# Differential attention on one core: keys and queries transposed in full precision and split afterwards, scores from three products over 64 rows, and a new order of the unit

## The chip, the cores and the metric

The kernel runs on 1 core of one Trainium2 chip. The metric is the device time of one execution in microseconds (us). The engines are named as in the profile: PE (TensorE, with PEld for its weight loads), DVE (VectorE), ACT (ScalarE), POOL (GpSimd) and SP, which only issues transfers here. Each engine works through its own instructions in the order in which the program has them; semaphores tie the engines together.

## What is computed

Two layers of a transformer with 1024 latent tokens and 256 context tokens of width 1024. In each layer one input projection feeds a Fourier mixer, a pooling mixer and differential attention; an output projection and a gated residual follow. The change lies in the attention, of which the reference says:

```python
def diff_attend(q, k, v, lam):
    s = jnp.einsum('bhmqd,bhmkd->bhmqk', q, k).astype(jnp.float32) * (QK_DIM ** -0.5)
    p = jax.nn.softmax(s, axis=-1)
    p = p[:, :, 0] - lam * p[:, :, 1]
    return jnp.einsum('bhqk,bhkd->bhqd', p.astype(v.dtype), v)
```

There are 4 heads; each has two maps (m = 0, 1) with queries and keys of 64 values, and values of 128. Before this, q and k are normalized (RMS over 64) and rotated. All inputs are float32.

## The kernel before

float32 data goes through TensorE in a reduced one-pass form (F32R). Where precision matters, a number is kept as hi + lo, two F32R parts, and a product is made of several matmuls that add up in PSUM: hi with hi, hi with lo, lo with hi.

**Stages of a layer**: projections for the gates and the mixers (whose work is not touched here), then the token-wise projections `proj_tok` in chunks of 256 columns: K0, K1, Q0, Q1, V0, V1. Each chunk works through pairs of token tiles (5 pairs for K and V); a pair takes 48 matmuls of 256 columns into one PSUM tile and then calls `post`, which issues the work on the result. Then attention runs in units.

**Keys**: `qk_post` normalizes and rotates a pair; one pair later `qk_late` scales it and writes, per head and map, `[hi | lo]` side by side into `ks` (128 tokens x 128). During the V chunks `k_trans` turns `ks` into `kT[2h+m]`, hi in rows 0 to 63 and lo in rows 64 to 127: 24 groups of up to four F32R transposes per layer, up to five groups behind each V pair (`v_chunk`). **Queries** go to DRAM (`qd`) and come back by query tile (`q_load`). For each unit `q_split` builds `[hi | lo | hi]` with three DVE instructions (L878 to L880) and `q_trans` makes four F32R transposes and one ACT copy (L892, L899).

**A unit** is one head of one tile of 128 queries against 1280 keys: 8 tiles x 4 heads, 32 units per layer. The first layer has two more, in which a context tile's four heads go together over 256 keys. `units` lists them, and `step(i)` issues for unit i (`cur`) its scores, row minima (the scores are negated) and exponentials, and for the units before it what comes later: `combine` (i-1) joins the two maps' exponentials, `p_trans` transposes the result in groups of 4, 4 and 2 tiles and `pv` multiplies by the values (i-2), `sub_norm` and `z_out` normalize and gate (i-2, i-3). When a query tile's four heads are done, `z_trans` and `z_low` transpose and split the gated result, and `out_proj` multiplies it by the output weights in pieces (`PIECES`, `ENDS`: first column, width, and how many steps after the last head).

`score(u, m)` makes one map: two products over all 128 rows, f = 0 and 1, in chunks of 512, 512 and 256 columns, 6 matmuls, so 12 in a unit. In `step` the two maps stand apart: scores of map 0 and its minimum first; transposes for the next unit, scores of map 1 and its minimum behind them.

**What sets the order**: the schedule is manual, each engine's queue is the order in which the code calls it. Two pools bind the engines: PSUM tiles `S` for scores (2 buffers, 3 banks each) and `x` for everything else (8 buffers up to the first V chunk, 2 from then on). A tile can be written again when its last reader is done.

## Time and profile before

| | us |
|---|---|
| median of 3 runs | 1451.82 (1447.77 to 1453.87) |
| profiled execution | 1448.99 |
| its span, first to last instruction | 1447.0 |
| first layer, minimum of unit 2 to minimum of unit 33 | 256.5 |
| second layer, minimum of unit 2 to minimum of unit 31 | 220.3 |
| PE busy in the span | 1381.8 (95%) |
| DVE busy in the span | 979.2 (68%) |

The profiled execution lies 2.8 us under the median of the runs. A matmul's end is modelled and includes the time to its result, so the pace of matmuls is read from start to start, not from their durations. "x6" in a row of the timeline means that six instructions in a row are merged; "[0.58 <-ACT t L938]" means that the engine sat idle for 0.58 us before, until that instruction released it.

### The profile page before, as it was taken

Reading aid. Unit: us, or ns where it says so; the run is one execution under the profiler, and the core shown is the slowest. Engines: PE = TensorE matmul, PEld = TensorE weight load, DVE = VectorE, ACT = ScalarE, POOL = GpSimd, SP = SyncE. Lnnn points to the kernel's source line nnn. Section 1 sums busy time; section 2 is a strip of 40 time slices with the busy share of each in tenths; the row PEclk is TensorE's granted clock in tenths of the full one; section 3 lists DMA queues with packets and bytes.
Section 4 is the critical chain, followed back from the end, with each engine's and each line's share of the span. In section 5 each row is a group of like instructions: output and inputs, shape, how many; then the busy total and the mean of one; then the engine's idle time right before and its main releaser. Section 6 shows DMA issues by size and latency. Waiting matters only on the chain.

```text
span 1447.0 us, 24063 instructions
## 1 busy us (share of the span) xinstructions
PE 1381.8 (95%) x9364; PEld 1240.6 (86%) x9364; DVE 979.2 (68%) x1553; ACT 567.6 (39%) x1230; POOL 775.9 (54%) x827
## 2 busy tenths in 40 slices
PE   7899999899999998999999899999999999999998
PEld 1688899779999987888888778988999998888887
DVE  2853366886895178798898654573464319989896
ACT  2632212101232265666665433121131227656663
POOL 2543222456785057667677842226887107766664
PEclk9899999999999999999999999999999999999999
DMA  9220242575123032112113321526412202111110
GB/s 354 101 90 32 85 149 91 187 266 166 60 88 117 1 103 81 66 45 74 45 45 112 104 66 38 205 80 213 148 44 85 78 22 67 45 45 45 59 59 30
DMA packets 65153, 137.07 MB, mean 95 GB/s; under 512 B 7312, under 2 KB 19728, under 8 KB 65040
## 3 DMA queue, kind: packets, MB, share of 16 engines
q1 hardware_dynamic: 49712, 108.82, 22.5%
q10 hardware_dynamic: 15328, 26.72, 5.3%
q8 instruction: 74, 1.21, 0.3%
q14 instruction: 39, 0.32, 0.1%
HBM read 105.63 MB, written 29.88 MB: 94 GB/s over the span
## 4 chain that ended last, share of the span: by engine, by line
PE 46%; DVE 21%; POOL 7%; issue 3%; ACT 2%; DMA 2%; ACTq 0%; POOLq 0%; SPq 0%; DVEq 0%
PE x L360 16%; DVE sm L923 6%; PE S L913 6%; PE x L1056 6%; PE x L993 5%; PE x L340 5%; PE x L753 3%; DVE e L1020 3%; PE x L977 2%; DVE t L952 1%; DVE t L980 1%; POOL e L759 1%; POOL sm L803 1%; DVE t L210 1%; PE x L892 1%
## 5 line engine op out<-in xcount | busy, mean ns | idle before, releaser
L360 PE MATMUL x<-wh,t 128*128 128x256 f32 x2432 | 445.9, 285 | 0.1
L360 PEld LDWEIGHTS x<-wh,t 128*128 128x128 f32 x2432 | 381.7, 192 | 1.8 <-issue 1.0
L360 PE MATMUL x<-wl,t 128*128 128x256 f32 x1216 | 344.7, 283 | 0.0
L923 DVE TENSOR_REDUCE sm<-S 128x1 f32<-128x1280 f32 (+1 forms) x132 | 194.8, 1476 | 72.2 <-PE S L913 72.0
L360 PEld LDWEIGHTS x<-wl,t 128*128 128x128 f32 x1216 | 233.7, 192 | 1.3 <-issue 1.2
L913 PE MATMUL S<-t,e 128*128 128x512 f32 (+1 forms) x768 | 180.9, 371 | 2.8 <-ACT e L899 1.4
L340 PE MATMUL x<-t,wh 128*128 128x512 f32 (+1 forms) x640 | 173.3, 381 | 8.8 <-DVE t L289 4.3
L938 ACT ACTIVATE t<-S,sm 128x1280 f32<-128x1280 f32 (+1 forms) x140 | 171.7, 1230 | 1.2 <-DVE sm L923 1.2
L993 PE MATMUL x<-t,t 128*128 128x128 f32 x1312 | 157.5, 275 | 3.3 <-DVE t L980 2.7
L993 PEld LDWEIGHTS x<-t,t 128*128 128x128 f32 x1312 | 153.7, 192 | 6.4 <-DVE t L980 2.9
L913 PEld LDWEIGHTS S<-t,e 128*128 128x128 f32 x768 | 126.3, 190 | 20.6 <-ACT t L938 2.0
L340 PEld LDWEIGHTS x<-t,wh 128*128 128x128 f32 x640 | 114.1, 192 | 31.6 <-POOL t L289 5.4
L318 POOL TENSOR_TENSOR wl<-st,wh 128x1024 fp32r<-128x1024 f32 x36 | 93.1, 2587 | 84.3 <-ACT wh L317 83.6
L961 POOL TENSOR_TENSOR t<-t,t 128x768 f32<-128x768 f32 (+1 forms) x64 | 116.2, 1816 | 5.3
L317 ACT ACTIVATE wh<-st 128x1024 fp32r<-128x1024 f32 x64 | 64.8, 1059 | 138.4 <-DMA xpart<-e 45.8
L977 PE MATMUL x<-ident,t 128*128 128x128 f32 x636 | 101.2, 274 | 5.7 <-DVE e L1059 4.1
L953 POOL TENSOR_SCALAR t<-t,sm 128x768 f32<-128x768 f32 x62 | 83.4, 1344 | 42.8 <-DVE sm L949 26.6
L753 PE MATMUL x<-wh,t 128*128 128x512 f32 x288 | 93.6, 404 | 8.5 <-DVE t L528 4.7
L1056 PE MATMUL x<-wh,e 128*128 128x512 f32 (+1 forms) x312 | 98.9, 384 | 2.6 <-ACT e L899 1.0
L340 PE MATMUL x<-t,wl 128*128 128x512 f32 (+1 forms) x320 | 100.2, 374 | 0.0
L210 DVE SCALAR_TENSOR_TENSOR t<-t,sc,t 128x512 f32<-128x512 f32 x98 | 90.8, 968 | 1.5 <-DMA t<-in_wmB_dram 1.1
L977 PEld LDWEIGHTS x<-ident,t 128*128 128x128 f32 x636 | 75.1, 141 | 15.9 <-DVE e L1059 4.5
(224 smaller groups left out, 2318.0 us busy)
## 6 DMA issues: line engine op xcount, KB each, us to landing
st<-in_w_in_dram SPq DMA_DIRECT2D x48, 512.0 KB, 4.0
t<-in_wmB_dram ACTq DMA_DIRECT2D x24, 512.0 KB, 5.4
xpart<-e ACTq DMA_DIRECT2D x36, 256.0 KB, 3.8
t<-xpart SPq DMA_DIRECT2D x18, 512.0 KB, 3.9
t<-in_wmS_dram SPq DMA_DIRECT2D x16, 512.0 KB, 8.5
st<-in_w_out_dram SPq DMA_DIRECT2D x16, 512.0 KB, 5.1
t<-in_x_dram SPq DMA_DIRECT2D x10, 512.0 KB, 10.3
e<-in_x_dram SPq DMA_DIRECT2D x20, 256.0 KB, 4.5
```

Source lines behind the costliest of these rows:

```text
L210: dve.scalar_tensor_tensor(a, w, sk, a, MULT, ADD)
L318: lo_eng[hf].tensor_tensor(lo[:, sl, :], st, hi[:, sl, :].bitcast(F32), SUB)
L340: pe.matmul(p[:, :m], lhsT=W[wi][:, k, ct * 128:ct * 128 + 128], rhs=H[k][hi][:, c0:c0 + m], start=(n == 0), stop=(n == 3 * KT - 1))
L360: pe.matmul(bank[:, i * 256:i * 256 + 256], lhsT=H[k][hi][:, j * 128:j * 128 + 128], rhs=W[wi][:, k, :], start=(n == 0), stop=(n == 3 * KT ...
L753: pe.matmul(ps, lhsT=zr[k][zi][:, j * 128:j * 128 + 128], rhs=W[wi][:, k, :], start=(n == 0), stop=(n == 11))
L913: pe.matmul(S[:, i * nk + c:i * nk + c + n], lhsT=s["qT"][i][:, m * 2 + f, :], rhs=kT[2 * h + m][:, k0 + c:k0 + c + n], start=(f == 0), st ...
L923: dve.tensor_reduce(nb, S[:, :nh * nk].rearrange("p (h k) -> p h k", h=nh), AX.X, ALU.min)
L938: act.activation(p[:, sl], S[:, sl], AF.Exp, bias=nb[:, i:i + 1], scale=-1.0, accum_out=ls[:, i:i + 1])
L961: pool.tensor_tensor(p[0][:, cut:end], p[0][:, cut:end], p[1][:, cut:end], ADD)
L977: pe.transpose(ps[:, i * 128:i * 128 + 128], s["p"][0][:, (t0 + i) * 128:(t0 + i + 1) * 128], ident)
L993: pe.matmul(o[:, i * 128:i * 128 + 128], lhsT=s["PT"][:, i * nkt + t, :], rhs=vv[h][:, kt0 + t, :], start=(t == 0), stop=(t == nkt - 1))
L1056: pe.matmul(ps[:, :m], lhsT=zz[:, k, :], rhs=Wa[hf][wi][:, k, w0:w0 + m], start=(n == 0), stop=(n == 11))
```

## The change

1. `qk_late` no longer splits the keys; it puts the scaled pair into a list. A new `k_trans`, called at the start of the next `qk_post`, makes four float32 transposes of it (both maps of a head lie in one 128x128 block), then ACT writes the hi part and DVE the lo part straight into `KH[h]` and `KL[h]`: rows 0 to 63 are map 0, rows 64 to 127 map 1. The transposes in the V chunks, `ks`, `identR`, `q_split` and the `qs` tiles are gone.
2. `q_trans` is called once per query tile, not per unit: four float32 transposes, one ACT copy (hi), one DVE subtraction (lo).
3. `score` makes both maps together: three products (hi hi, hi lo, lo hi) over 64 rows each, the two maps in turn, 18 matmuls in a unit instead of 12. The built program gives the matmuls of map 0 the rows 0 to 63 of the array and those of map 1 the rows 64 to 127.
4. `step` has another order, `out_proj` four pieces of 256 columns, one in each of the steps 2 to 5 after a tile's last head, and `z_trans` and `z_low` move to the end of a step. The gates (`g_load`) are loaded four steps later. `e2` has 10 buffers instead of 9.

```diff
-    e2p = tc.alloc_tile_pool(name="e2", bufs=9)
+    e2p = tc.alloc_tile_pool(name="e2", bufs=10)
...
+        def k_trans():
+            if later:
+                p, c, t1 = later.pop(0)
+                ps = PX()
+                for hh in range(2):
+                    for i in range(2):
+                        o = (2 * hh + i) * 128
+                        pe.transpose(ps[:, o:o + 128], t1[:, i, 2 * hh:2 * hh + 2, :].rearrange("p m e -> p (m e)"), ident)
+                for hh in range(2):
+                    hi, lo = [K[2 * c + hh][:, 256 * p:256 * p + 256] for K in (KH, KL)]
+                    b = ps[:, 256 * hh:256 * hh + 256]
+                    act.activation(hi, b, AF.Copy)
+                    dve.tensor_tensor(lo, b, hi.bitcast(F32), SUB)
...
-                for m in range(4):
-                    kd = ks[4 * c + m][:, 2 * p:2 * p + 2, :]
-                    act.activation(kd[:, :, 0:64], t1[:, :, m, :], AF.Copy)
-                    (dve if m % 2 else pool).tensor_tensor(kd[:, :, 64:128], t1[:, :, m, :], kd[:, :, 0:64].bitcast(F32), SUB)
+                else:
+                    later.append((p, c, t1))
...
+        def q_trans(j):
+
+            ps = PX()
+            for h in range(NH):
+                pe.transpose(ps[:, h * 128:h * 128 + 128], st[j]["q"][:, h * 128:h * 128 + 128], ident)
+            hi, lo = parts(j)
+            act.activation(hi.rearrange("p a b -> p (a b)"), ps, AF.Copy)
+            dve.tensor_tensor(lo.rearrange("p a b -> p (a b)"), ps, hi.rearrange("p a b -> p (a b)").bitcast(F32), SUB)
+            st[j]["Q"] = hi, lo
...
+                for n, (q, k) in enumerate(((0, KH), (0, KL), (1, KH))):
                     for c in range(0, nk, 512):
...
+                        w = min(512, nk - c)
+                        for m in range(2):
+                            r = slice(64 * m, 64 * m + 64)
+                            pe.matmul(S[m][:, i * nk + c:i * nk + c + w], lhsT=Q[q][r, h, :],
+                                      rhs=k[h][r, k0 + c:k0 + c + w], start=(n == 0), stop=(n == 2))
...
-        PIECES = [(0, 512, 2), (512, 512, 3)]
-        ENDS = {} if full else {6: [(0, 256, 3), (256, 256, 5), (512, 256, 5), (768, 256, 6)],
-                                7: [(0, 512, 2), (512, 256, 3), (768, 256, 3)]}
+        PIECES = [(c, 256, 2 + c // 256) for c in range(0, D, 256)]
+        LAST = {7: [(0, 512, 2), (512, 512, 3)]} if full else {7: [(0, 512, 2), (512, 256, 3), (768, 256, 3)]}
+        ENDS = () if full else (6, 7)
...
-                for _ in range(5):
-                    if k_groups:
-                        k_trans(*k_groups.pop(0))
```

The new body of `step`, in its three parts (what is left out in the third are the output pieces that are due):

```python
            if old:
                p_trans(old, 0)
                p_trans(old, 4)
            if prev and i > 1:
                combine(prev)
            if cur:
                score(cur)
            if old:
                p_trans(old, 8)
            if cur:
                row_max(cur, 0)
                row_max(cur, 1)
            if done:
                z_out(done)
            yield
            ...
            if cur:
                expo(cur, 0)
            if old:
                pv(old)
            if cur:
                expo(cur, 1)
            if old:
                sub_norm(old)
            yield
            ...
            if 1 in fin:
                z_trans(fin[1])
                z_low(fin[1])
            if i + 1 < N and units[i + 1][1] in (0, -1):
                q_trans(units[i + 1][0])
```

PE in the second layer, before, at the end of one step and the start of the next, in a step without an output piece (L977 transposes for PV, L913 scores, L892 query transposes, L993 PV, `x` and `S` the PSUM tiles):

```order
L977 MATMUL x_14108<-ident,t_2409_13936 128x128 x2
L993 MATMUL x_14120<-t_1893_11492,t_2441_14060 128x128 x10
L977 MATMUL x_14136<-ident,t_2434_14037 128x128 x4
L913 MATMUL S_14142<-t_1925_11808,e_2447_14087 128x512 x2
L913 MATMUL S_14142<-t_1925_11808,e_2447_14087 128x256
L913 MATMUL S_14142<-t_1925_11808,e_2447_14087 128x512 x2
L913 MATMUL S_14142<-t_1925_11808,e_2447_14087 128x256
L977 MATMUL x_14149<-ident,t_2434_14037 128x128 x4
L1026 MATMUL x_14155<-ident,e_2236_13264 128x128 x4
L892 MATMUL x_14171<-identR,qs_14113 128x128 x4
```

PE in the second layer, after, at the end of a step with `z_trans` (L1007) and the start of the next (L1036 the output piece, L958 transposes for PV, L894 scores):

```order
L1036 MATMUL x_14470<-wh_12536,e_2329_14103 128x256
L1036 MATMUL x_14470<-wl_12537,e_2329_14103 128x256
L1036 MATMUL x_14470<-wh_12536,e_2330_14104 128x256
L1007 MATMUL x_14487<-ident,e_2297_13963 128x128 x4
L958 MATMUL x_14497<-ident,t_2388_14356 128x128 x4
L958 MATMUL x_14503<-ident,t_2388_14356 128x128 x4
L894 MATMUL S_14519<-t_1756_10622,e_2352_14203 128x512
L894 MATMUL S_14520<-t_1756_10622,e_2352_14203 128x512
L894 MATMUL S_14519<-t_1756_10622,e_2352_14203 128x512
L894 MATMUL S_14520<-t_1756_10622,e_2352_14203 128x512
L894 MATMUL S_14519<-t_1756_10622,e_2352_14203 128x256
L894 MATMUL S_14520<-t_1756_10622,e_2352_14203 128x256
```

The scores now need both `S` buffers at once, the map alternates with every matmul, and three groups of four transposes (or an output piece and two of them) stand ahead of them and share two `x` buffers.

ACT before, in the step whose next one needs `z_trans` (L938 exponentials, L996 copy of PV's result, L982 copies for PV, L1029 hi of `z_trans`, L1004 squares, L899 copy of the query transposes):

```order
L938 ACTIVATE t_2549_14485,sm_14486<-S_14435,sm_14448 128x1280
L996 ACTIVATE t_2503_14304<-x_14488 128x128
L938 ACTIVATE t_2552_14500,sm_14501<-S_14467,sm_14474 128x1280
L982 ACTIVATE t_2554_14503<-x_14517 128x512
L1029 ACTIVATE e_2559_14528<-x_14523 128x512
L1004 ACTIVATE t_2503_14304,sm_14531<-t_2503_14304 128x128
L899 ACTIVATE e_2565_14544<-x_14539 128x512
```

ACT after, in a step with `q_trans` (L919 exponentials, L977 copy of PV's result, L985 squares, L875 hi of the queries, L963 copies for PV):

```order
L919 ACTIVATE t_2342_14159,sm_14160<-S_14130,sm_14154 128x1280
L977 ACTIVATE t_2299_13967<-x_14162 128x128
L919 ACTIVATE t_2345_14174,sm_14175<-S_14131,sm_14156 128x1280
L985 ACTIVATE t_2299_13967,sm_14177<-t_2299_13967 128x128
L875 ACTIVATE e_2352_14203<-x_14198 128x512
L963 ACTIVATE t_2355_14209<-x_14216 128x512
L963 ACTIVATE t_2355_14209<-x_14252 128x256
```

The copy that frees the `x` buffer of `z_trans` or `q_trans` stands behind both exponentials and the squares.

## Rows read from the trace of the kernel before

**Rows 1.** Windows, attention of both layers: us; busy (instructions) of PE, PEld, DVE, ACT, POOL; clock; DMA

```profile
518.83:775.37 256.54, 242.37 (x1671) 216.96 (x1669) 224.18 (x346) 168.06 (x394) 174.64 (x230) 0.99 0.21 69
1196.50:1416.80 220.30, 215.46 (x1503) 193.37 (x1501) 200.74 (x305) 142.97 (x300) 152.80 (x188) 1.00 0.15 50
```

**Rows 2.** Timeline of DVE in the second layer: start us, us, engine, line, operation

```profile
1281.94 1.48 DVE L923 TENSOR_REDUCE sm<-S 128x1 f32<-128x1280 f32 x1
1283.34 1.51 DVE L1020 SCALAR_TENSOR_TENSOR e<-t,sm,e 128x128 f32<-128x128 f32 x1
...
1285.38 0.68 DVE L980 COPY t<-x 128x512 f32<-128x512 f32 x1
...
1285.98 1.47 DVE L923 TENSOR_REDUCE sm<-S 128x1 f32<-128x1280 f32 x1
...
1292.54 1.48 DVE L923 TENSOR_REDUCE sm<-S 128x1 f32<-128x1280 f32 x1
```

**Rows 3.** Timeline of PE in the same units

```profile
1284.01 1.40 PE L913 MATMUL S<-t,e 128*128 128x512 f32 x6
...
1285.25 0.60 PE L977 MATMUL x<-ident,t 128*128 128x128 f32 x4
...
1287.72 0.38 PE L977 MATMUL x<-ident,t 128*128 128x128 f32 x2
...
1287.94 2.40 PE L993 MATMUL x<-t,t 128*128 128x128 f32 x20
...
1290.18 0.60 PE L977 MATMUL x<-ident,t 128*128 128x128 f32 x4
```

**Rows 4.** Windows, L360 alone, between two V pairs: us, PE, PEld, clock

```profile
502.02:507.79 5.77, 5.73 (x48) 5.52 (x46) 1.00 0.01 3
```

**Rows 5.** Timeline of ACT, and of `z_low` on DVE, in the second layer

```profile
1283.86 0.28 ACT L996 ACTIVATE t<-x 128x128 f32<-128x128 f32 x1 [0.54 <-PE x L993]
1284.03 1.32 ACT L938 ACTIVATE t<-S,sm 128x1280 f32<-128x1280 f32 x1
...
1285.89 0.60 ACT L982 ACTIVATE t<-x 128x512 f32<-128x512 f32 x1 [0.16 <-PE x L977]
...
1293.36 0.60 ACT L1029 ACTIVATE e<-x 128x512 fp32r<-128x512 f32 x1 [0.34 <-PE x L1026]
...
1293.99 0.69 DVE L1034 TENSOR_TENSOR e<-x,e 128x512 fp32r<-128x512 f32 x1
```

**Rows 6.** Timeline, scores that wait for an exponential to free their buffer

```profile
515.72 1.34 ACT L938 ACTIVATE t<-S,sm 128x1280 f32<-128x1280 f32 x1
...
517.21 1.43 PE L913 MATMUL S<-t,e 128*128 128x512 f32 x6 [0.58 <-ACT t L938]
```

**Rows 7.** Timeline of DVE at the end, an output piece of 256 columns

```profile
1434.77 0.42 DVE L1059 TENSOR_TENSOR e<-x,t 128x256 f32<-128x256 f32 x1
```

**Rows 8.** Timeline of ACT, copies behind the first and fifth pair of V0, both layers

```profile
446.02 0.66 ACT L1097 ACTIVATE t<-x 128x256 f32<-128x256 f32 x2 [1.74 <-PE x L360]
...
479.78 0.66 ACT L1097 ACTIVATE t<-x 128x256 f32<-128x256 f32 x2 [5.57 <-PE x L360]
...
1128.46 0.66 ACT L1097 ACTIVATE t<-x 128x256 f32<-128x256 f32 x2 [3.21 <-PE x L360]
...
1157.40 0.66 ACT L1097 ACTIVATE t<-x 128x256 f32<-128x256 f32 x2 [5.57 <-PE x L360]
```

**Rows 9.** Timeline of DVE, the scaling of keys in `qk_late`, ten pairs apart, first layer

```profile
355.89 0.69 DVE L786 TENSOR_TENSOR e<-e,sm 128x512 f32<-128x512 f32 x1 [0.96 <-POOL e L817]
...
417.38 0.68 DVE L786 TENSOR_TENSOR e<-e,sm 128x512 f32<-128x512 f32 x1
```

**Rows 10.** Timeline of PE's weight loads where the used part of the array changes

```profile
17.52 0.09 PEld L157 LDWEIGHTS x<-t,sc 128*2 128x2 f32 x1 [0.35 <-issue]
18.47 0.32 PEld L166 LDWEIGHTS x<-ident,e 2*128 2x128 f32 x4 [0.86 <-issue]
```

**Rows 11.** Timeline of POOL while `z_out` stands on DVE

```profile
1282.88 1.82 POOL L961 TENSOR_TENSOR t<-t,t 128x768 f32<-128x768 f32 x1
```

More of the change, by code (lines that the diff above doesn't have):

```diff
@@ L827, in layer @@
             W = w_get()
-            for m in range(4):
-                ks[4 * c + m] = T5([128, 10, 128], F32R)
+            for _ in range(2):
+                KH.append(T5([128, NTOK], F32R))
+                KL.append(T5([128, NTOK], F32R))
             proj_tok(H, W, 5, qk_post(1, c))
@@ L834, in layer @@
         qk_late()
+        k_trans()
         st = {}
         def q_load(j):
[L838 to L839 removed]
+            q = (T5 if j >= 8 else E2)([128, 512])
             sp.dma_start(q, qd[l][j])
[L841 to L859 removed]
+            st[j] = dict(q=q)
@@ L883, in q_trans, with parts @@
[L883 to L900 removed]
+        def parts(j):
+            if j >= 8:
+                t = T5([128, 8, 128], F32R)
+                return t[:, 0:4, :], t[:, 4:8, :]
+            return [E2([128, 4, 128], F32R) for _ in range(2)]
@@ L1087, in layer @@
         vv = []
-        k_groups = [(m, t0) for m in range(8) for t0 in (0, 4, 8)]
         def v_chunk(c, W, between=None):
@@ L1121, in step @@
                 p_trans(old, 0)
+                p_trans(old, 4)
+            if prev and i > 1:
+                combine(prev)
             if cur:
-                score(cur, 0)
+                score(cur)
             if old:
-                p_trans(old, 4)
-            if 2 in fin:
-                z_trans(fin[2])
-            if 2 in fin and 0 <= i - 3 < N:
-                sub_norm(units[i - 3])
+                p_trans(old, 8)
             if cur:
                 row_max(cur, 0)
-            if 2 in fin:
-                z_low(fin[2])
+                row_max(cur, 1)
+            if done:
+                z_out(done)
             yield
@@ L1137, in step @@
                     q_load(j)
-            if nxt:
-                q_trans(nxt)
-            if prev and i > 1:
-                combine(prev)
-            if cur:
-                score(cur, 1)
-            if cur:
-                row_max(cur, 1)
-            if old:
-                p_trans(old, 8)
-            if 0 <= i - 3 < N:
-                z_out(units[i - 3])
-            if nxt:
-                q_trans(nxt, 1)
-            if i + 2 < N:
-                q_split(units[i + 2])
+                if j in first and first[j] + 1 == i:
+                    g_load(j)
             if cur:
                 expo(cur, 0)
+            if old:
+                pv(old)
+            if cur:
+                expo(cur, 1)
+            if old:
+                sub_norm(old)
             yield
             for d, j in sorted(fin.items(), key=lambda f: f[1]):
-                for c0, m, late in ENDS.get(j, PIECES):
-                    if d == late:
+                for c0, m, at in LAST.get(j, PIECES):
+                    if d == at:
                         out_proj(j, c0, m)
-            if i + 2 < N:
-                q_split(units[i + 2], 1)
+            if 1 in fin:
[3 more added lines that the diff above has]
+                q_trans(units[i + 1][0])
             while rms:
@@ L1167, in step @@
                     break
-            if old:
-                pv(old)
-            if cur:
-                expo(cur, 1)
-            if old and 1 not in fin:
-                sub_norm(old)
-            if full and 3 in fin:
-                rms.append(tile_rms(fin[3]))
+            if full:
+                for d, j in fin.items():
+                    if d == LAST.get(j, PIECES)[-1][2]:
+                        rms.append(tile_rms(j))
             yield
```

91 lines of the change are left out of this document (17 added, 74 removed).

## The prediction

> **What bounds the kernel now.** I read the windows of the two attention stretches first, since most of the change lies there. The reader is to see that no engine alone sets the end: in the second layer's 220.3 us PE is busy for 215.5 and DVE for 200.7, and the two stretches together are 476.8 of a span of 1447 [rows 1]. The 29 steps of the second layer take 7.6 us each, the 31 of the first 8.3.
>
> Then the timelines of DVE and PE for one unit without an output piece. It lasts 6.56 us from minimum to minimum, and DVE never pauses in it; `z_out` alone holds it for 1.44 us, and it ends 0.15 us after POOL's long addition [rows 2, 11]. PE's part of such a unit is: scores 1.24 us for six matmuls, so 2.48 for both maps; transposes 0.22 for two, so 0.11 each; PV 2.24 [rows 3]. In units with an output piece PE is the one without a pause. So a gain has to shorten PE's and DVE's unit at once, and it must not build a new chain through both.
>
> **The change part by part.** All sums are made against the profiled execution, 1449.0 us; the median of the runs is 2.8 us higher.
>
> *Score time.* A set of chunks (512, 512, 256) takes 1.24 us before [rows 3]. Now there are three products with two maps, six such sets on half the rows each. If two matmuls on different halves of the array run side by side, this is three sets, 1.86 us; one after the other it is six, 3.72; before it was 2.48. The trace of before has no two matmuls on different rows at once, so both are bounds, and their distance is large: 1.86 us x 66 units. I take the side-by-side end: neighbours differ in rows and write different PSUM banks, and in the projections a weight load is already hidden beside every matmul (48 in 5.77 us, though loads and matmuls are each busy for almost all of it) [rows 4], so what PE needs to overlap two instructions is there. The Trainium skill, "TensorE: Matmul & The Clock Gate", Part 3 on packing small matmuls, says that matmuls on different row groups start some 4 ns apart and run concurrently; by it the sum would be the 1.86 of above. No row here shows it.
>
> *Changing the array's shape.* Every unit now goes from 128 rows to 64 and back. The nearest rows are at the program's start, where a matmul with 2 used columns is followed by one with 2 used rows: weight loads there come every 0.43 us or so (0.09 and 0.35 idle), but the load of the new shape starts only 0.95 us after the last one [rows 10]. A load there runs one matmul ahead, so the last matmul starts 0.43 us after its load and streams for 0.43; 0.09 us are lost beyond it. I take 0.09 for each change of shape, 0.18 per unit on PE; the ends are 0 and 0.17 (the whole 0.16 us that a score's result needs after the last start, 1284.01 + 1.40 against 1285.25 [rows 3]). The Trainium skill, "TensorEngine Tiling (Array Packing)", Key Properties, speaks against the change here: "Changing tiling mode (not just tile) drains the TensorE". The rows agree in kind; by a full drain at both changes the sum would be the upper end.
>
> *The new step, without a tile's end.* Start at the first score matmul, T = 0. Scores end at 1.86; the minimum of map 0 starts 0.2 later at 2.06, that of map 1 1.40 later at 3.46 and ends at 4.94 [rows 2, 3]. The first exponential runs from 3.55 and keeps ACT for 1.30; PV's copy follows, and 0.17 after it the second exponential, at 5.02 [rows 5]. The next scores need its buffer and start 1.49 after it, at 6.51 [rows 6]. PE in the meantime: 1.86, two transposes 0.22, PV 2.24, twelve matmuls of 256 columns 1.44 (5.77 / 48 each [rows 4]), the next unit's first four transposes 0.44: 6.20. The second four need the `x` buffer of the output piece, whose result lands at 5.92 and which DVE reads for 0.42 [rows 7]: they start at 6.42 and end at 6.86. So PE is last, 6.86, with two changes of shape 7.04; without an output piece it is the exponential, 6.51 and one change, 6.60. DVE has room: without the query splits (between `z_out` and the next copy at 1285.38 [rows 2]), and with `z_out` behind both minima, where POOL's addition is over, it is no longer the bound. What it costs if that cover goes: `combine` now stands ahead of the minimum, and a POOL instruction may hold it as `z_out` was held, up to 0.45 us in about every other unit.
>
> *The step at a tile's end* (`z_trans`) *or ahead of a new tile* (`q_trans`). Four more transposes take PV's `x` buffer. Their ACT copy stands behind both exponentials and the squares: from an exponential to the next copy are 1.86 - 0.16 = 1.70 us, so it starts at 6.72, ends at 7.32, and DVE's lo part runs from 7.35 to 8.04 [rows 5]. Only then is the buffer free for the next unit's second four transposes, 8.08 to 8.52, and the scores stand behind them in PE's queue. So 8.52, with one change 8.61. This is the new wait that replaces the old one: PE stands idle for some 1.2 us (the first four transposes end at 6.86) for a copy that has nothing to do with the scores.
>
> *Sum over attention.* In the second layer, 29 steps: 14 with `z_trans` or `q_trans`, 12 plain, 3 without a piece: 14 x 8.61 + 12 x 7.04 + 3 x 6.60 = 224.8, against 220.3: +4.5. In the first, 31 steps: 18 and 13, and 4 plain steps with a second piece (1.44 each), and about 2 us for the context units' eight short exponentials: 155.0 + 91.5 + 5.8 + 2 = 254.3, against 256.5: -2.2. Together +2.
>
> *Outside.* The V chunks lose the key transposes. Four pairs there take 33.8 us in the first layer and 28.9 in the second [rows 8], where matmuls alone would take 4 x 5.77: 10.7 and 5.9 us for 20 of 24 groups; the last four at the second layer's rate 1.2 each: -19 in all. The key chunks gain 20 groups of four float32 transposes, 0.44 each: +8.8. PE now also waits there for the scaled keys; in the first layer DVE needs 61.5 us for ten pairs [rows 9] and PE 57.7, so this wait is at most 3.8 us and lies inside the 4.4 us that PE spends there on transposes; +4 if it does not. The first two units of each layer run inside the V1 chunk, which PE bounds: four sets become three, -1.2 us a layer, -2.4. The last tile's output pieces keep their length; the loads of the gates, moved four steps later, land in a few us with a step or more to spare: nothing. `identR`'s copy: nothing. Together -12.6, say -13.
>
> So 1449 + 2 - 13 = **1438 us**, 1% under the median.
>
> **The rivals.**
>
> *A, cheaper than taken:* the change of shape costs nothing. Then plain steps are 6.86 (6.51 without a piece), the others 8.52: 3.7 us less in the second layer, 3.9 in the first, about 1430. For it: the queue can be filled while PE waits for the exponential. Against: the weight load at the program's start did wait [rows 10].
>
> *B, slower through the weights:* each score matmul has its own weight load. A transpose with its load costs 0.11 us [rows 3], and if loads for both halves share one path, a pair of 256 columns takes 0.22 instead of 0.12: +0.3 us per unit. With the upper end of the change of shape and some of `combine`'s hold that is 0.4 to 0.5 us x 66 units: +28, about 1466. It decides as soon as a unit's scores take over 2.1 us or so: below it the gains outside cover it. For it: the score chain (scores, two minima, exponential) has no slack in it any more, so every tenth of a us comes back 66 times, 6.6 us. Against: loads hide well beside full matmuls [rows 4].
>
> *C, the change does not do what it says:* the halves do not run side by side. +1.86 x 66 = 123 us: about 1561. For it: nothing in the trace shows such concurrency. Against: only that nothing forbids it.
>
> **How the numbers follow.** Chances: the forecast (1433 to 1447) 0.40, A or better (under 1433) 0.16, B (1447 to 1495) 0.29, C 0.15. The likeliest is the forecast, 1438. The range reaches from 1422 (A, with a few us more in the first layer, whose units are the most disturbed now) to 1490 (B with the key wait and `combine`'s hold); it leaves out C and little at the lower end. A measurement of this kernel tells about 0.5%, 7 us, from no change. Faster by more than that is under 1444.5: three quarters of the forecast and A, 0.46. Within it, up to 1459: 0.10 from the forecast and 0.10 from B: 0.20. Slower: the rest of B and C, 0.34. The signs are mixed; the forecast's own range is 1433 to 1447.
>
> **What would show it.** Right: 18 score matmuls whose starts come in pairs and which end some 1.9 us after the first; steps of about 7.0 and 8.6 us in turn, two and two; before the second four transposes of the long steps PE idle for over 1 us, released by DVE's lo part; V0 pairs at 5.8 us; DVE with pauses. Wrong: score starts evenly spaced over 3.7 us (C), or pairs at an even 0.22 whatever their width (B); long steps no longer than the short ones, which would mean that the copy behind the exponentials frees its buffer earlier than I hold; PE stalls in the key chunks of the first layer.

## The result

The changed kernel takes 1490.08 us (median of four runs, 1486.70 to 1491.31), the kernel before 1452.78 on the same chip: a ratio of 1.026, 95% interval 1.023 to 1.029. The forecast was 1438 in a range of 1422 to 1490; the change makes the kernel slower by 37 us, and the time lies just above the range's upper end. The profiled execution has a span of 1487.7 us against 1447.0, so 40.7 us are to be found. The page's first part (busy us, share of the span, instructions) and its chain of waits by engine, with the kernel before's chain below it:

```profile
PE 1367.3 (92%) x9828; PEld 1211.1 (81%) x9828; DVE 876.0 (59%) x1372; ACT 525.6 (35%) x1112; POOL 743.8 (50%) x817
...
PE 51%; DVE 11%; ACT 9%; issue 5%; POOL 4%; DMA 2%; ACTq 0%; SPq 0%; DVEq 0%; POOLq 0%
...
PE 46%; DVE 21%; POOL 7%; issue 3%; ACT 2%; DMA 2%; ACTq 0%; POOLq 0%; SPq 0%; DVEq 0%
```

DVE and ACT have room, and DVE's share of the chain has halved; but ACT's has grown from 2% to 9%, so a fifth of the span still runs through the two.

The first reading cuts both spans at the same events: the copy behind the first pair of V0 (446.02 and 1128.46 in [rows 8]), the first minimum of a layer's third unit, and that of its last unit (the ends of the windows in [rows 1]). "Forecast" is the prediction's own term for the stretch.

| stretch | before, us | after, us | difference | forecast |
|---|---|---|---|---|
| start to V0, layer 1 (key and query chunks at its end) | 446.0 | 463.6 | +17.6 | +4.4 |
| V0 and V1, first two units, layer 1 | 72.8 | 62.6 | -10.2 | -13.1 |
| attention, layer 1 | 256.5 | 271.0 | +14.4 | -2.2 |
| from there to V0, layer 2 | 353.1 | 363.5 | +10.4 | +4.4 |
| V0 and V1, first two units, layer 2 | 68.0 | 61.8 | -6.3 | -8.3 |
| attention, layer 2 | 220.3 | 236.9 | +16.6 | +4.5 |
| last unit to the end | 30.2 | 28.3 | -1.9 | 0 |

Three lines hold most of the miss of 51 us: the way to V0 in layer 1, and both attentions. The first of them is larger than it looks. Up to the first key matmul the two programs issue the same matmuls, yet the profiled execution after came there at 316.43 us and the one before at 322.29 (the other profiles below lie between 317.7 and 322.4); from there to V0 it is 147.2 us against 123.7, so the key and query chunks cost 23.4 us more, not 17.6.

The windows of the two attentions and, below them, two parts of layer 2's (columns as in [rows 1]: us; busy time and instructions of PE, PEld, DVE, ACT, POOL; granted clock; DMA share; GB/s):

```profile
526.24:797.19 270.95, 238.21 (x1946) 206.53 (x1946) 182.31 (x276) 153.75 (x363) 173.09 (x249) 0.97 0.17 55
1222.47:1459.41 236.94, 213.17 (x1738) 183.50 (x1738) 162.53 (x241) 131.23 (x279) 152.37 (x204) 0.97 0.13 44
1222.47:1283.66 61.19, 51.02 (x374) 42.43 (x374) 39.25 (x53) 34.19 (x70) 40.97 (x49) 0.89 0.11 35
1283.66:1459.41 175.75, 162.16 (x1365) 141.07 (x1366) 123.28 (x188) 97.05 (x209) 111.39 (x156) 1.00 0.14 48
```

DVE's work fell from 200.7 to 162.5 us in layer 2, as meant (`z_out`, out of the way of POOL's long addition, from 1.43 to 0.39 us in the mean), and PE's from 215.5 to 213.2; yet the stretch is longer. The loss is not spread evenly: the seven steps up to 1283.66 take 61.19 us where the forecast's terms give 52.7 (three long ones at 8.61, one plain at 7.04, three at 6.60), with PE idle for 10 us and a clock of 0.89. The 22 steps behind them take 175.75, and the forecast 172.2.

A late step with `z_trans`, on PE, ACT and DVE (timelines: start us, us, engine, line, operation, wait before it and its releaser; L1007 and L873 are the transposes of z and q, L1009 and L1014 the high and low part of z, L958 the transposes for PV, L894 scores, L974 PV):

```profile
1358.63 0.60 PE L1007 MATMUL x<-ident,e 128*128 128x128 f32 x4
1359.30 0.65 PE L958 MATMUL x<-ident,t 128*128 128x128 f32 x4
1360.99 0.63 PE L958 MATMUL x<-ident,t 128*128 128x128 f32 x4 [1.03 <-DVE e L1014]
1361.55 2.00 PE L894 MATMUL S<-t,e 64*128 64x512 f32 x18
1363.48 0.44 PE L958 MATMUL x<-ident,t 128*128 128x128 f32 x2
1363.76 2.40 PE L974 MATMUL x<-t,t 128*128 128x128 f32 x20
...
1359.45 0.60 ACT L1009 ACTIVATE e<-x 128x512 fp32r<-128x512 f32 x1
...
1360.15 0.69 DVE L1014 TENSOR_TENSOR e<-x,e 128x512 fp32r<-128x512 f32 x1 [0.91 <-ACT e L1009]
1360.76 0.68 DVE L961 COPY t<-x 128x512 f32<-128x512 f32 x1
```

This is the step that the prediction drew: 18 scores in 2.00 us where [rows 3] had 1.40 for six, PE waiting 1.03 us for the low part, then the second four transposes, then the scores. The steps come two and two, 7.22 and 7.22, then 8.79 and 8.73.

Early in layer 1 the same chain looks like this, in the step in which a context unit's results are squared (L985 squares, L316 the next weights' cast to float32r; then PE in the same step, and the windows on both sides of PE's wait, PE alone: us, busy time and instructions, clock, DMA):

```profile
566.32 0.31 ACT L985 ACTIVATE t<-t 128x128 f32<-128x128 f32 x1
...
567.48 1.05 ACT L316 ACTIVATE wh<-st 128x1024 fp32r<-128x1024 f32 x1
568.43 0.59 ACT L1009 ACTIVATE e<-x 128x512 fp32r<-128x512 f32 x1
...
565.18 0.66 PE L958 MATMUL x<-ident,t 128*128 128x128 f32 x4
569.89 1.01 PE L958 MATMUL x<-ident,t 128*128 128x128 f32 x4 [4.05 <-DVE e L1014]
570.83 3.17 PE L894 MATMUL S<-t,e 64*128 64x512 f32 x18
...
561.69:569.89 8.20, 3.33 (x26) 1.00 0.17 64
569.89:574.04 4.15, 4.15 (x23) 0.59 0.23 80
```

Four squares and a cast stand ahead of z's copy, which starts 3 us after the transposes that it reads. PE waits 4.05 us, and then works at 0.59 of full clock in the mean, near the lower of its two levels (1.2 and 2.4 GHz): the scores take 3.17 us instead of 2.00.

Ahead of V0 in layer 1, PE stood still at the first key transposes (timeline, and windows of PE alone):

```profile
334.45 0.28 PE L359 MATMUL x<-wh,t 128*128 128x256 f32 x1
350.47 0.90 PE L786 MATMUL x<-ident,e 128*128 128x128 f32 x3 [15.75 <-DVE e L798]
...
350.40:357.00 6.60, 6.53 (x38) 0.66 0.00 0
357.00:365.00 8.00, 8.00 (x70) 1.00 0.01 3
```

15.75 us, and some 2 us more at 0.66 of full clock behind it. In the kernel before PE was busy without a pause from 344 to 446 us.

### The profile page after: what moved, and what is told of

It reads as the page before. It is cut to its first block, busy times and chain, and to the rows that moved or that the text cites. A ratio compares the mean times of both kernels' runs of the same rounds, so it can differ in the third digit from the quotient of the medians.

```text
span 1487.7 us, 24648 instructions
## 1 busy us (share of the span) xinstructions
PE 1367.3 (92%) x9828; PEld 1211.1 (81%) x9828; DVE 876.0 (59%) x1372; ACT 525.6 (35%) x1112; POOL 743.8 (50%) x817
## 4 chain that ended last, share of the span: by engine, by line
PE 51%; DVE 11%; ACT 9%; issue 5%; POOL 4%; DMA 2%; ACTq 0%; SPq 0%; DVEq 0%; POOLq 0%
PE x L359 21%; PE S L894 9%; ACT t L919 5%; PE x L974 5%; PE x L339 5%; PE x L1036 4%; DVE sm L904 3%; PE x L958 3%; PE x L751 3%; DMA t<-in_wmB_dram 1%; DVE t L209 1%; POOL t L288 1%; DVE e L1039 1%; ACT t L985 1%; DVE wl L317 1%
## 5 line engine op out<-in xcount | busy, mean ns | idle before, releaser
L904 DVE TENSOR_REDUCE sm<-S 128x1 f32<-128x1280 f32 (+1 forms) x132 | 189.5, 1478 | 123.6 <-PE S L894 123.6
L919 ACT ACTIVATE t<-S,sm 128x1280 f32<-128x1280 f32 (+1 forms) x140 | 172.3, 1234 | 52.5 <-DVE sm L904 51.4
L974 PE MATMUL x<-t,t 128*128 128x128 f32 x1312 | 161.0, 279 | 6.4 <-DVE t L961 6.4
L974 PEld LDWEIGHTS x<-t,t 128*128 128x128 f32 x1312 | 155.2, 196 | 7.3 <-DVE t L961 6.6
L958 PE MATMUL x<-ident,t 128*128 128x128 f32 x636 | 109.7, 288 | 54.8 <-DVE e L1014 19.6
L894 PE MATMUL S<-t,e 64*128 64x512 f32 (+1 forms) x1152 | 140.0, 382 | 4.1 <-ACT t L919 3.4
L958 PEld LDWEIGHTS x<-ident,t 128*128 128x128 f32 x636 | 69.0, 143 | 91.0 <-POOL sm L993 37.8
L894 PEld LDWEIGHTS S<-t,e 64*128 64x128 f32 x1152 | 102.1, 196 | 32.1 <-issue 9.9
L963 ACT ACTIVATE t<-x 128x512 f32<-128x512 f32 (+1 forms) x130 | 63.9, 493 | 177.0 <-PE x L958 177.0
L942 POOL TENSOR_TENSOR t<-t,t 128x768 f32<-128x768 f32 (+1 forms) x64 | 115.0, 1798 | 5.3
L316 ACT ACTIVATE wh<-st 128x1024 fp32r<-128x1024 f32 x64 | 64.9, 1062 | 131.8 <-DMA xpart<-e 73.3
L1036 PE MATMUL x<-wh,e 128*128 128x256 f32 (+1 forms) x488 | 105.3, 298 | 0.8 <-ACT e L1009 0.7
L989 POOL TENSOR_SCALAR sm<-sm,sm 128x1 f32<-128x1 f32 x64 | 17.2, 269 | 165.5 <-ACT t L985 160.1
## 6 DMA issues: line engine op xcount, KB each, us to landing
t<-in_x_dram SPq DMA_DIRECT2D x10, 512.0 KB, 10.2
```

What stands on the lines that cost most here:

```text
L316: act.activation(hi[:, sl, :], st, AF.Copy)
L894: pe.matmul(S[m][:, i * nk + c:i * nk + c + w], lhsT=Q[q][r, h, :], rhs=k[h][r, k0 + c:k0 + c + w], start=(n == 0), stop=(n == 2))
L904: dve.tensor_reduce(nb, S[:, :nh * nk].rearrange("p (h k) -> p h k", h=nh), AX.X, ALU.min)
L919: act.activation(p[:, sl], S[:, sl], AF.Exp, bias=nb[:, i:i + 1], scale=-1.0, accum_out=ls[:, i:i + 1])
L942: pool.tensor_tensor(p[0][:, cut:end], p[0][:, cut:end], p[1][:, cut:end], ADD)
L958: pe.transpose(ps[:, i * 128:i * 128 + 128], s["p"][0][:, (t0 + i) * 128:(t0 + i + 1) * 128], ident)
```

## The experiments

Theory W: the score's sums hold, and the time went into PE's queue, where work that waits for other engines now stands ahead of matmuls that don't. Its rival in each stretch is given with the run. All ratios are to the kernel before on the same chip, with 95% intervals. Gains and losses in us are differences to the changed kernel's 1490.08. The runs lie on several chips, on which the kernel before has medians from 1448.6 to 1452.8 us, so a difference of 4 us is no more than the noise.

**Key transposes three pairs later.** Each group is issued when three more are waiting (cut, and one more `e2` buffer):

```
-            if later:
+            if len(later) > depth:
...
-                k_trans()
+                k_trans(3 if qk == 1 else 0)
```

> The changed kernel, but in the key chunks each group of key transposes is issued three pairs later (one more e2 buffer). Theory W (the time went into PE's queue: work that waits for other engines now stands ahead of matmuls that do not): the 15.75 us wait of PE in layer 1 for the first scaled keys goes, and with it the slow matmuls after it (0.67 of full clock over 6 us, 2 us): 1490 becomes about 1472, 1.3 percent over the kernel before. Rival G (the key pipeline itself is late, and the wait only moves to the full set of PSUM banks or to the query chunks): within 5 us of 1490.

1474.23 us, 1.016 (1.0128 to 1.0191): 16 us less. PE no longer waits there and the clock stays up; in the changed kernel the 123.6 us from 340 us to V0 had a clock of 0.94 (windows, PE, PEld, DVE, ACT, POOL):

```profile
340.00:450.00 110.00, 110.00 (x923) 109.88 (x922) 94.20 (x157) 27.21 (x52) 90.89 (x76) 1.00 0.29 92
```

From the first key matmul to V0 it is 128.2 us now, 4.5 more than before the change, where the forecast had 4.4. So the whole wait was PE's order, and none of it came back in this stretch.

**The weights' cast behind the copy of z or q.** `if n == 1 and i >= 4` becomes `n == 2`.

> The changed kernel, but the float32r cast of the next weights (1.06 us on ACT, four a layer) is issued at the end of a step, behind the copy of z or q, instead of between the second exponential and that copy. Theory W: five of the eight casts stand in steps that already wait for that copy, 1.06 us each, 5.3 us; and the idle time of PE there is what lowers its clock (0.77 and 0.80 in two steps of layer 2), which gives back up to 3 us in each of these: 1490 becomes 1476 to 1485. Rival P (POOL's 2.4 us for the low part of the weights is what makes these steps long, through the long addition on the same engine): 1488 to 1493.

1485.99 us, 1.0252 (1.022 to 1.0284): 4 us less, between the two theories and within the noise, so only the steps tell something. In layer 2 the two worst steps fall from 11.70 and 11.51 to 10.55 and 9.55. This alone doesn't tell the cast from POOL's work, which moved with it.

**The cast ahead of the first exponential**, `n == 0`, where ACT waits for the minimum anyway. The kernel with all repairs, of which the expectation speaks, is the last one below.

> The changed kernel with one edit: the weights' cast is issued ahead of the first exponential, where ACT waits for the minimum. In the kernel with all repairs this edit brought 10 us. If the cast ahead of the copy of z or q, with the slower clock after PE's wait, is what makes the first steps of each layer long in the changed kernel itself, the two steps of 11.5 us in layer 2 fall below 10 and the time to 1476 to 1484. If POOL's low part of the weights does it, the time stays within 3 us of 1490.

1484.30 us, 1.024 (1.0219 to 1.0261): 6 us less, just above the range expected, and the intervals of the two ratios overlap. Layer 2's first seven steps take 54.84 us instead of 61.19 at a clock of 0.96; the two worst fall from 11.70 and 11.51 to 10.37 and 8.73, so one of them not below 10. POOL is as busy there as before (39.8 and 41.0 us), but its low part of the weights moves with the cast here as well, so the run doesn't tell the two apart either. The changed kernel's trace shows more: in its step of 11.70 us PE waits twice (PE; then ACT's cast and its copy of z, `z_out` on DVE in L1001, and POOL's long addition in L942):

```profile
1257.71 0.33 PE L1007 MATMUL x<-ident,e 128*128 128x128 f32 x1 [1.71 <-DVE e L1001]
1260.18 1.09 PE L958 MATMUL x<-ident,t 128*128 128x128 f32 x4 [1.71 <-DVE e L1014]
...
1257.77 1.06 ACT L316 ACTIVATE wh<-st 128x1024 fp32r<-128x1024 f32 x1
1258.71 0.60 ACT L1009 ACTIVATE e<-x 128x512 fp32r<-128x512 f32 x1
...
1255.92 1.74 DVE L1001 SCALAR_TENSOR_TENSOR e<-t,sm,e 128x128 f32<-128x128 f32 x1
...
1255.70 1.81 POOL L942 TENSOR_TENSOR t<-t,t 128x768 f32<-128x768 f32 x1
```

The second wait follows the cast. The first follows POOL: its low part of the weights (2.37 us from 1252.37) stands ahead of the addition, and `z_out`, caught behind that, takes 1.74 us instead of 0.34. That first wait stays with the cast behind the copy (1.69 us) and falls to 0.20 with the cast ahead of the exponential. So both theories hold a part in this step. In layer 1 nothing is gained (183.3 us for twenty steps, 183.8 before); there the squares of the context units and of the finished tiles stand ahead of the copy as well, but no run moved them.

**DVE makes the high part of z and q.** `act.activation(hi, ps, AF.Copy)` becomes `dve.tensor_copy(hi, ps)`, twice.

> The changed kernel, but DVE instead of ACT makes the high part of z and q out of PSUM, right behind the transposes, so that it does not stand behind the second exponential and the squares. Theory W: the steps of 8.75 us (31 in both layers) lose the 1.0 us that PE waits for the low part, part of it again to DVE's 0.68 us for the copy: 0.6 to 1.2 us each, 1490 becomes 1453 to 1471. Rival S (these steps are long because scores and changes of shape take longer than costed, and the wait is only what is left over): within 8 us of 1490.

1470.86 us, 1.0145 (1.0117 to 1.0173): 19 us less, in theory W's range, but not where expected. The late long steps only fall from 8.75 to between 8.63 and 8.71; the gain is in the first twenty steps of layer 1 and the first seven of layer 2. Windows of both attentions:

```profile
530.82:785.70 254.88, 232.71 (x1946) 202.04 (x1946) 195.51 (x294) 144.44 (x345) 173.46 (x249) 0.99 0.18 59
1211.27:1440.80 229.53, 209.58 (x1738) 180.91 (x1738) 173.58 (x254) 124.42 (x265) 151.33 (x203) 0.99 0.14 46
```

254.9 us is the forecast's 254.3, 229.5 is 4.7 above its 224.8. The first agreement is in part luck, since steps of up to 10.23 us stand beside some of 6.46 to 7.20 there. So ACT's queue made most of the early steps' excess, and in the late ones it is not ACT's queue: DVE, too, starts only when the transposes and its read of the output piece are done.

**Maps not alternating.** Inside a product the three matmuls of map 0 come first, then those of map 1.

> The changed kernel, but inside each product the three matmuls of map 0 come first, then the three of map 1, so that neighbours use the same rows of the array. If matmuls run side by side only where neighbours use different rows, one pair in three still overlaps: scores take 3.1 to 3.7 us instead of 2.0, 66 units, 1490 becomes 1560 to 1600. If the array overlaps them whatever the order, or if the alternation was not what made 18 matmuls end in 2.0 us: within 8 us of 1490.

1494.11 us, 1.0298 (1.0262 to 1.0333): within 4 us. The scores of a unit end as soon as before:

```profile
1349.56 2.03 PE L894 MATMUL S<-t,e 64*128 64x512 f32 x18
```

Alternation is not needed. That left open whether matmuls run side by side at all.

**Both maps on the same rows.** `r = slice(64 * m, 64 * m + 64)` becomes `slice(0, 64)`.

> The changed kernel, but both maps are computed from rows 0 to 63 of queries and keys, so map 1 is left out and map 0 is computed twice, with the same number and shape of matmuls. If the 18 score matmuls of a unit end in 2.0 us because those on different rows run side by side, they now run one after the other: 3.7 us, 1.7 more for each of 66 units, 1490 becomes about 1600. Rival H (a matmul on 64 rows simply takes half the time, whatever stands beside it): scores stay at 2.0 us and the time within 8 us of 1490.

1631.53 us, 1.1247 (1.1218 to 1.1275), 141 us more, and the scores take

```profile
1489.74 3.75 PE L894 MATMUL S<-t,e 64*128 64x512 f32 x18
```

The same 18 matmuls need 3.75 us on the same rows and 2.02 on two halves: they do run side by side, over a distance of three matmuls as well as of one. Late plain steps take 8.93 us instead of 7.22, the 1.7 expected; most of the rest of the 141 us lies in the early steps, with a clock of 0.90 over the first attention. Rival C of the prediction is out, and the Trainium skill's rule of "TensorE: Matmul & The Clock Gate", Part 3, on packing small matmuls into row groups holds here.

**Two more changes of shape.** The two transposes behind the scores stand between the second and the third product.

> The changed kernel, but the two transposes that follow the scores stand between the second and the third of the three products, so that the array's shape changes four times a unit and not twice; all instructions are the same. By the trace of the changed kernel two changes cost 0.19 us a unit (0.56 us from the start of four transposes of 0.44 to the first score, 1.93 us for scores of 1.86): 66 units, 12.5 us more, 1490 becomes 1500 to 1505, and the plain steps 7.4 instead of 7.2. Rival Z (changes of shape cost nothing, the 0.19 us belongs to the ends of scores and transposes): at most 3 us more.

1523.69 us, 1.0495 (1.0475 to 1.0515): 33 us more, against 12.5 expected. Plain steps take 7.61 us instead of 7.22, long ones 9.29 to 9.37 instead of 8.73 to 8.80. On PE:

```profile
1399.30 1.43 PE L897 MATMUL S<-t,e 64*128 64x512 f32 x12
1400.66 0.44 PE L961 MATMUL x<-ident,t 128*128 128x128 f32 x2
1401.03 0.85 PE L897 MATMUL S<-t,e 64*128 64x512 f32 x6
```

From the first score to PV it is 2.51 us (PV starts at 1401.81), where the changed kernel has 2.21 (1361.55 to 1363.76): 0.15 us for each change of shape, and 0.20 by the plain step's 0.39; twice what the expectation had read for two changes off the changed kernel's trace. The long steps' 0.57 holds the transposes too. Such a step hangs on the minima and exponentials behind the scores, and the first minimum now starts 2.61 us after the first score instead of 2.04 (1363.59 in the changed kernel):

```profile
1401.91 2.89 DVE L907 TENSOR_REDUCE sm<-S 128x1 f32<-128x1280 f32 x2 [1.60 <-PE S L897]
```

So the price is near the upper end of the prediction's bounds (0.17), not the 0.09 taken. "Changing tiling mode (not just tile) drains the TensorE", says the Trainium skill, "TensorEngine Tiling (Array Packing)", Key Properties; the 0.15 to 0.20 us agree with it in size, since the prediction put a full drain at 0.17, but whether the drain is full they don't show.

**The PSUM buffer of z and q freed earlier, first try.** DVE copies it whole beside ACT's copy, and the low part comes from SBUF.

> The changed kernel, but beside ACT's copy of the high part DVE copies z or q whole out of PSUM, and makes the low part from that copy in SBUF, so that the PSUM buffer is free one DVE operation (0.69 us) earlier and no longer behind a chain of two. Theory B (what makes the steps of 8.75 us long is this buffer: four transposes, high part, low part in a row before the next unit's second four transposes; not ACT's queue, since DVE making the copy left the late steps at 8.65 to 8.71): the low part's 0.7 to 0.9 us goes from each of 31 steps, 8.75 becomes 7.8 to 8.1, 1490 becomes 1462 to 1470. Rival D (DVE's work before the minima is then last, since it has 0.69 us more of it): steps stay above 8.5, 1483 to 1495.

1496.57 us, 1.0314 (1.0298 to 1.0331): 6 us more, but theory B was not tried by it. DVE's copy waited for the semaphore of ACT's copy out of the same buffer and started behind it:

```profile
1366.82 0.69 DVE L1013 COPY e<-x 128x512 f32<-128x512 f32 x1 [0.89 <-ACT e L1011]
1367.55 0.94 DVE L1018 TENSOR_TENSOR e<-e,e 128x512 fp32r<-128x512 f32 x1
```

The buffer came free as late as before. Together with the late keys and the moved cast the same edit shows the other two gains only:

> Key transposes three pairs later, the weights' cast at the end of the step, and the PSUM buffer of z and q freed early, together. Theory W and B: 16 us, 4 us and 20 to 28 us come off 1490, since they are in different stretches or, in the long steps with a cast, overlap by 2 or 3 us: 1442 to 1452, the level of the kernel before (1449) or a little below. Rival D (DVE is last in the long steps): 1464 to 1475.

1472.33 us, 1.0153 (1.0135 to 1.0171): in rival D's range, but for the reason just shown and not for rival D's.

**Second try: read once.** DVE copies out of PSUM, ACT makes the high part and POOL the low part from that copy; alone and with the late keys (shortened):

```
-            act.activation(hi, ps, AF.Copy)
-            dve.tensor_tensor(lo, ps, hi, SUB)
+            t = E2()
+            dve.tensor_copy(t, ps)
+            act.activation(hi, t, AF.Copy)
+            pool.tensor_tensor(lo, t, hi, SUB)
```

> The changed kernel, but z and q are read out of PSUM once, by a DVE copy right behind their transposes; ACT makes the high part from that copy in SBUF and POOL the low part. The attempt before this one did not free the buffer earlier, since DVE's copy stood behind ACT's read of the same buffer (0.89 us). Theory B (the buffer's chain of transposes, high part, low part makes the long steps): the buffer is free some 0.7 us after the transposes, PE's wait of 0.95 to 1.03 us before the second four transposes goes, late long steps fall from 8.75 to 7.7 to 8.0, the early ones from 9 to 12 to below 9: 31 steps, 25 us, and 15 to 23 us early: 1490 becomes 1440 to 1455. Rival D (something else is as late: POOL with another 1.3 us, or the minima behind DVE's copies): late long steps above 8.5, 1465 to 1475 as when DVE made the copy.

> The same, with the key transposes three pairs later as well. The two lie in different stretches, so the gains add: 16 us below the run with the single read. Theory B: 1424 to 1440, faster than the kernel before (1449) by 0.6 to 1.7 percent. Rival D: 1449 to 1459.

1488.34 us, 1.0262 (1.0237 to 1.0286), and 1468.94, 1.0131 (1.0104 to 1.0158), both above the ranges of either theory. Half of theory B holds: PE's wait is gone. But rival D takes its place, in a step with `q_trans` (L935 and L944 are DVE's and POOL's parts of the combination, L878 the low part):

```profile
1366.55 1.42 PE L960 MATMUL x<-ident,t 128*128 128x128 f32 x8
1367.96 1.44 PE L896 MATMUL S<-t,e 64*128 64x512 f32 x12
1370.08 0.86 PE L896 MATMUL S<-t,e 64*128 64x512 f32 x6 [0.67 <-POOL e L878]
...
1368.84 1.73 DVE L935 SCALAR_TENSOR_TENSOR t<-t,sm,t 128x512 f32<-128x512 f32 x1
...
1368.74 1.28 POOL L878 TENSOR_TENSOR e<-e,e 128x512 fp32r<-128x512 f32 x1
```

All eight transposes run without a pause, and the scores start 0.75 to 0.9 us sooner in the step. Then the third product waits for POOL, and the combination's 0.75 us on DVE become 1.73, since it starts while POOL's subtraction has 1.18 us left. Long steps take 8.20 and 8.65 us, and the early ones up to 12.89.

**The two repairs that were measured, together**: late keys, and DVE's high part.

> DVE makes the high part of z and q out of PSUM, and the key transposes stand three pairs later: the two repairs that have each been measured (19 and 16 us), together. If they lie in different stretches the gains add: 1455, 0.4 percent over the kernel before. If the earlier start of the attention costs elsewhere: up to 1465.

1451.42 us, 1.0008 (0.9994 to 1.0022). The gains add, 16 + 19 and 4 more, and the change stands level with the kernel before. The two edits take back 39 of the 51 us that the forecast missed.

**Low part on DVE, in another place.** As read once, but the low part stands behind the next unit's first copy and ahead of the combination; with late keys, and with the cast in both places:

> Key transposes three pairs later, z and q read out of PSUM once by DVE (which let PE go on without the wait), and the low part on DVE again, but behind the next unit's copy of its first transposes and ahead of the combination, where ACT has finished the high part. In the run with POOL's low part PE's wait before the second four transposes was gone, but POOL's 1.28 us stood beside DVE's combination, which took 1.73 instead of 0.75 us and delayed the minima. Theory B: long steps fall to 7.8 to 8.0 us; 31 steps, 23 to 28 us below the run with DVE's copy and late keys (1451): 1423 to 1432, faster than the kernel before by 1.2 to 1.8 percent. Rival D (DVE's four operations before the minima are last): long steps stay at 8.4 to 8.7, 1446 to 1455.

> The same, with the weights' cast issued ahead of the first exponential, where ACT waits for the minimum (0.83 us in the changed kernel), and not behind the second one. If the long first steps of each layer (9 to 12 us) come from the cast that stands ahead of the high part on ACT, these steps fall to 8 to 8.5 us: 4 to 8 us below the run without this edit. If they come from POOL's low part of the weights (2.4 us beside the combination), they stay: within 3 us of it.

1447.51 us, 0.9979 (0.9967 to 0.9991), and with the cast ahead of the exponential 1437.25 us, 0.9914 (0.9889 to 0.9939): 0.2% and 0.9% below the kernel before. In the first of the two, late long steps fall to 8.05 us, close to theory B's 7.8 to 8.0, yet the time misses its 1423 to 1432: steps of 10 to 11 us are left early in both layers. The cast's place, with POOL's low part moving along, is worth 10 us here, more than expected. The seventh and eighth unit of layer 2, first without and then with it:

```profile
1223.36:1243.74 20.38, 16.97 (x117) 13.77 (x118) 16.91 (x20) 11.15 (x22) 15.73 (x17) 0.83 0.24 78
```

```profile
1214.46:1229.70 15.24, 13.99 (x117) 11.81 (x118) 13.93 (x21) 11.19 (x22) 14.56 (x16) 1.00 0.31 104
```

The same 117 matmuls with nearly as much work on POOL, 5 us apart: 2 us of wait less, and 3 us of PE's own time by the clock. In the late long steps DVE is now the engine without a pause. In `ordered_cast0` it reads q, copies for PV, makes the low part, and combines, up to the minimum:

```profile
1317.38 0.69 DVE L883 COPY e<-x 128x512 f32<-128x512 f32 x1
1318.11 0.69 DVE L970 COPY t<-x 128x512 f32<-128x512 f32 x1
1318.84 1.23 DVE L874 TENSOR_TENSOR e<-e,e 128x512 fp32r<-128x512 f32 x1
1319.99 0.15 DVE L937 RECIPROCAL sm<-sm 128x1 f32<-128x1 f32 x1
...
1320.43 0.75 DVE L942 SCALAR_TENSOR_TENSOR t<-t,sm,t 128x512 f32<-128x512 f32 x1
1321.10 2.88 DVE L913 TENSOR_REDUCE sm<-S 128x1 f32<-128x1280 f32 x2
```

## Why the prediction was wrong, step by step

**Score time: right.** Taken 1.86 us side by side; the trace has 1.93 to 1.96 from the first score to the next transposes, one change of shape in it. Rival C fell. (The prediction writes that a set of three chunks takes 1.24 us; in [rows 3] that is one map's six matmuls, so two sets. Its 1.86 and 3.72 are three and six sets of 0.62, and right.)

**Late steps: right in kind, 0.16 us too short each.** Two and two, 7.2 and 8.75 us against 7.04 and 8.61, with the wait where it was put. The term that was off is the change of shape, 0.09 taken and 0.15 to 0.20 measured. By the upper end of its bounds, 0.17, the steps come out at 7.20 and 8.69, and the 22 late steps of layer 2 at 174.8 instead of 172.2, against 175.75. Over both layers that term is some 7 us. The prediction had chosen by [rows 10], one change at the program's start.

**The cause given for the long steps: only half right.** "Their ACT copy stands behind both exponentials and the squares" is what the trace shows (6.71 us after the first score, 6.72 forecast). But taking the copy off ACT freed 0.1 us only. The buffer's last reader is DVE's low part, and the chain from transposes over high and low part to it is as long on DVE alone; reading the buffer once is what removed PE's wait.

**The early steps: the largest error, some 23 us** (of which the change of shape has 3). The failed step is that the prediction costed every step of a kind by one late step. In the first twenty steps of layer 1 and the first seven of layer 2, ACT also has the weights' casts, the squares of context units and finished tiles, all ahead of the copy that frees PE's buffer. PE's wait ahead of the scores, 1.0 us in the late long steps, was between 1.6 and 4.1 us in ten of these steps; over the 4 us behind it the clock stood at 0.50 to 0.63 in seven of the ten and at 1.00 in three. POOL has a part in it: "with `z_out` behind both minima, where POOL's addition is over" holds in the late steps, but not where POOL's low part of the weights delays the addition, as in the step of 11.70 us. In the kernel before, the same casts of 1.06 us stood on ACT, and PE's clock stayed at 0.99 and 1.00 [rows 1]. The forecast allowed 2 us for the context units, and named no cast.

**The key chunks: the failed step by itself.** The step "this wait is at most 3.8 us and lies inside the 4.4 us" compared two rates, 61.5 us and 57.7 us for ten pairs [rows 4, 9]. What counts for an instruction that stands in PE's queue is the lag: in the kernel before the first scaled key came at 355.89 us [rows 9], while PE, which eight PSUM buffers let run ahead, was in its sixth pair (from 351.94). The prediction had the first figure in its rows and didn't set the second beside it. Measured: 15.75 us of wait and some 2 us of slow clock, so 19 of the 23.4 us; in layer 2 PE did not wait, and the transposes cost what was forecast (114.2 us from the first key matmul to V0, 109.7 before).

**Outside otherwise: near.** The V chunks and first units gave 16.5 us of 21.4. The way from one attention to layer 2's key chunks took some 6 us more than forecast, after PE's waits of 6.36 us (for DVE's copy of transposes, where the kernel before waited 2.70) and 3.38 us (for split weights, no such wait before) at its start; no run was made on it, and its cause stays open.

**Rival B** names the right side and size (1447 to 1495), but by luck, not by its mechanism: weight loads for two halves do not get in each other's way (18 matmuls with their loads in 1.95 us). Of its three parts only the upper end of the change of shape came true; the combination's hold did not show in the late steps of the changed kernel, whose 0.75 us are undisturbed. The key wait, which the range's upper end of 1490 took in, was real, but four times as long.

## What to carry to other kernels

An instruction that waits for another engine costs its lag when it is put into a queue, not the difference of two rates; so read when its input is first ready, and how far ahead the queue's engine runs there. Cost a step where it is most crowded, too: an operation that frees a buffer waits behind everything its engine has in that stretch, and what it costs PE can come back a second time by the clock. Where a buffer holds PE up, read it out once, at once, and make the rest from the copy, in an order that leaves the other engines' chain its slack.

## What the hardware showed

The 18 score matmuls end equally early whether the two halves of the rows take turns with every matmul or with every third (2.02 and 2.03 us); all on one half they take 3.75. A change between 64 and 128 rows costs PE 0.15 to 0.20 us each time. After waits of 4 and 16 us PE worked at 0.59 and 0.66 of full clock over the next 4 and 7 us; 18 scores then took 3.17 us instead of 2.00. Shorter waits went both ways: of eight between 1.6 and 2.8 us five were followed by 4 us at 0.50 to 0.63 and three by a clock of 1.00, and those of 0.95 to 1.05 in the late steps left it at 1.00.

DVE operations with two tensors in SBUF that started inside a wide POOL operation ended only after it. In the kernel before, 50 of 62 `z_out` started inside POOL's addition of 768 columns, with 1.35 to 1.66 us of it left, and took 1.50 to 1.80 us instead of 0.34: they end 0.15 us behind it [rows 2, 11]. The combination and the low part end some 0.55 us behind POOL: 1.73 us instead of 0.75 with 1.18 left of POOL's subtraction, and 1.23 instead of 0.69 with 0.68 left of an addition. A combination that started before POOL's wide operation kept its 0.75 us (55 times in the changed kernel).
